# A two-layer diffusion trunk on one core: weights laid out in tile order by the host, and mirrored token tiles gathered by row numbers

## The chip, the core and the metric

The kernel runs on one core of a Trainium2 chip. The core has five engines that run their own instruction streams: TensorE (PE, matrix products; its weight loads are PEld), VectorE (DVE), ScalarE (ACT), GpSimd (POOL) and SyncE (SP), which here only issues DMAs. Sixteen DMA engines move data between the device memory (DRAM) and the on-chip memory. The metric is the device time of one execution in microseconds, and the median of the runs is taken.

## What is computed

The reference is a trunk of two layers over 512 latent tokens of 1024 features, with 256 context tokens. Layer 0 mixes tokens with a bidirectional state-space model (S5) on half of the features and neighbourhood attention on the other half; layer 1 mixes with a two-dimensional Fourier transform and a linear map. After each mixer there is a squared-ReLU MLP with 4096 hidden features. Cut to what matters here:

```python
def fourier_mix(h, w_f):
    hf = jnp.fft.fft2(h.astype(jnp.float32), axes=(1, 2), norm='ortho').real
    return hf.astype(h.dtype) @ w_f

def sqrelu_mlp(x, w1, w2):
    return jnp.square(jax.nn.relu(x @ w1)) @ w2

    # in each layer (sh, sc, g: slices of silu(c) @ w_mod[layer] + b_mod[layer])
        hl = modulate(rms_norm(h, norm_g[layer, 0]), sh1, sc1)
        ...                                  # out_l: S5 and attention, or fourier_mix(hl, w_fourier)
        h = h + g1[:, None, :] * rms_norm(out_l, norm_g[layer, 1])
        hf = modulate(rms_norm(h, norm_g[layer, 2]), sh2, sc2)
        h = h + g2[:, None, :] * rms_norm(sqrelu_mlp(hf, w_ff1[layer], w_ff2[layer]), norm_g[layer, 3])
```

All of it is float32.

## The kernel before

Every float32 product is made of three products in PE's float32r format: each operand is split into a high part and a low rest, and `mm3` (L105 to L108) adds high times high, high times low and low times high. Weights stream through the on-chip memory in chunks of 1 MB, a tile of 128 partitions by 2048 numbers. `Weights.pair` issues the load on SP (L54), lets ACT cast the high part (`whi`, L66) and DVE subtract it for the low part (`wlo`, L70). For some chunks (five of `w_in`, one of `w_out`, chunk 0 of `w_ff1` in each layer) ACT writes the negative high part (L68) and a DMA that POOL issues (L72) adds the weights onto it a second time from DRAM, in place of DVE. A chunk is cut from the plain matrix, so a partition's 8 KB come as eight rows of 1 KB (`w_in`, `w_ff1`) or four of 2 KB (`w_glu`, `w_out`, `w_ff2`). The modulation columns of the first norm (`wm`, L272) come as sixteen loads of 512 KB, in rows of 512 bytes.

The order of the instructions on each engine is chosen by a scheduler that simulates the program when it is built; each engine then runs its own list in that order. A DMA on SP or POOL is issued in the order of that engine's list, too.

The Fourier mixing of layer 1 is written with half-size transforms that use mirror symmetries. At the end of the first MLP each of the four token tiles of the residual `h` is written to DRAM (`hd`, L1137, in `fold`), normed into the tile `mf`, and folded on DVE (L1112 to L1117, L1145; a memset of one column by POOL, L1147). `stage1` (L1160, L1171) multiplies the folds by a token table into the PSUM tiles `pst`, then `feat` (L1213, L1215) multiplies by a feature table (`td<-tabD`, L1190) into `pa` and `pn`. Their results are split into `abh` and `abl`, and first columns are kept as `nyc` (L1224). `ny` is the split last row (`stack3`, L1074 to L1082). `stage3` multiplies by the linear map into `pq` and `pp` (L106 to L108, and L1264 with `ny`).

The map is used in four parts q = 0 to 3 of 256 columns, as the sums and differences of its rows l and 1024 - l. `mapw` loads a part with five DMAs, rows of `w_fourier` and of its reversed copy `wfr` (L1090 to L1093), and a memset (L1094); takes the difference `ws` (L1098) and the sum (L1101), on DVE for q = 1 and on POOL for the others; splits both (L183); and loads one more row (L1105). Part 1 goes into a piece of the tile `td`, part 3 (`w`, the tile `w3`) into the room of `mf`.

The mixing's output leaves in an order in which half of the tokens are mirrored (tokens 256, 511, 510 and so on). So the residual is brought into that order: a DRAM copy `hr` of the second half in reverse (L1184) is read back into tiles 1 and 3 of `h` (L1249, L1250, L1252); tiles 0 and 2 are read from `hd` (L1248, L1251).

Of the kernel before, what the change touches and what calls it, by code (L numbers as in the profile page):

```python
# [34 lines left out]
class Weights:  # L35
    """Streams float32 weights in chunks and splits each exactly into two float32r parts."""
# [23 lines left out]
    def pair(self, src, n0, n1, pair=None, dma=False, parts=1):  # L60
        """dma: the low part is summed by a DMA, where VectorE is short of time."""
# [32 lines left out]
def trunk(tc, I, out, dump=None):  # L94
# [15 lines left out]
    with es:  # L110
# [7 lines left out]
        def psum(**bufs):  # L118
            """Cuts the PSUM banks anew: the number of each kind."""
# [18 lines left out]
        # ------------------------------------------------ constants  # L138
# [32 lines left out]
        def rstd(src, junk):  # L171
            """1 / rms of the rows of src [128, 1024]; junk is overwritten."""
# [40 lines left out]
        def gemv_row(p, layer, slot, dst, norm, plus):  # L213
            """dst [128, 1024], on every partition: (vector (+ 1)) * gain of that norm."""
# [18 lines left out]
        def gemv_cols(p, layer, slot, dst, b, g):  # L233
            """dst [128, 8], feature-major: the vector, or (vector + 1) * gain."""
# [11 lines left out]
        # ------------------------------------------------ layer 0  # L246
# [9 lines left out]
        def win(i):  # L256
            return W.pair(I["w_in"][0, :, i * 256:(i + 1) * 256].rearrange("(k p) n -> p k n", p=128), 8, 256,
                          dma=i in (5, 6, 7, 2, 3), parts=4)
# [35 lines left out]
        with pool("s5t", side="right") as st:  # L294
# [41 lines left out]
            # the rotation of 8 steps, as a fraction of 2^32; backward rows turn the other way  # L336
# [45 lines left out]
        # ------------------------------------------------ norm, modulation, S5's input  # L382
# [12 lines left out]
        def mod_cols(k):  # L395
            """Ac, Bc of feature block k: the block's modulation for both streams."""
# [120 lines left out]
        # ------------------------------------------------ S5: 8 blocks of 4 groups  # L517
        st_ = {}

        def s5_params(b):  # L520
            """Chunk operators of block b: transposed input map Qt, readout CA, local convolution M, rotations R."""
# [12 lines left out]
            if b in (1, 3, 5):  # before the queries come  # L534
# [57 lines left out]
        def s5_scan(b):  # L592
            """Runs block b: chunk inputs, scan over chunks, readout."""
# [85 lines left out]
        # ------------------------------------------------ neighbourhood attention  # L679
# [94 lines left out]
        def glu_weights():  # L774
            wo["glu"] = W.pair(I["w_glu"].rearrange("(k p) n -> p k n", p=128), 4, 512)
# [10 lines left out]
        # ------------------------------------------------ the rest of it, GLU  # L786
# [45 lines left out]
        def wout(i, pair=None):  # L832
            hf, kk = divmod(i, 2)
            return W.pair(I["w_out"][kk * 512:kk * 512 + 512, hf * 512:hf * 512 + 512]
                          .rearrange("(k p) n -> p k n", p=128), 4, 512, pair, i == 0, parts=2 if i < 3 else 1)
# [16 lines left out]
        # ------------------------------------------------ output projection, MLPs, Fourier mixing  # L852
# [9 lines left out]
        def residual(t, src, G, early=False):  # L862
            """h[t] += rms_norm(src) * gate, the gains folded into G; src is overwritten."""
# [17 lines left out]
        def halves(t):  # L881
            """A [128, 4104] tile as [half of the tokens, feature block, token]."""
# [42 lines left out]
        def load1(layer, c, dma=False):  # L925
            return W.pair(I["w_ff1"][layer, :, c * 256:(c + 1) * 256].rearrange("(k p) n -> p k n", p=128), 8, 256,
                          dma=dma)

        def load2(layer, p_, hf):
            return W.pair(I["w_ff2"][layer, p_ * 512:(p_ + 1) * 512, hf * 512:(hf + 1) * 512]  # L930
                          .rearrange("(k p) n -> p k n", p=128), 4, 512)

        # output projection, with the first MLP's input following each token tile
# [491 lines left out]
```

## Time and profile before

| | |
|---|---|
| median of 3 runs | 1275.31 us |
| the runs | 1271.62, 1275.31, 1276.59 us |
| span of the profiled execution | 1266.4 us |
| mean TensorE clock granted in it | 0.971 |
| PE busy | 1172.3 us (93%) |
| DVE, ACT, POOL busy | 794.3, 502.8, 100.6 us |
| moved by DMA | 171.76 MB in 127259 packets, of which 90956 under 2 KB |

The span runs from the first to the last instruction of one execution that the hardware profiler recorded, and all views below are of it. The median of the timed runs is 8.9 us longer than that span. PE is the busiest engine; where it is idle, the profile says which instruction it waited for and which engine or DMA released it.

### The profile page before, as it was taken

Reading aid. Unit: us, or ns where it says so; the run is one execution under the profiler, and the core shown is the slowest. Engines: PE = TensorE matmul, PEld = TensorE weight load, DVE = VectorE, ACT = ScalarE, POOL = GpSimd, SP = SyncE. Lnnn points to the kernel's source line nnn. Section 1 sums busy time; section 2 is a strip of 40 time slices with the busy share of each in tenths; the row PEclk is TensorE's granted clock in tenths of the full one; section 3 lists DMA queues with packets and bytes.
Section 4 is the critical chain, followed back from the end, with each engine's and each line's share of the span. In section 5 each row is a group of like instructions: output and inputs, shape, how many; then the busy total and the mean of one; then the engine's idle time right before and its main releaser. Section 6 shows DMA issues by size and latency. Waiting matters only on the chain.

```text
span 1266.4 us, 15594 instructions
## 1 busy us (share of the span) xinstructions
PE 1172.3 (93%) x6090; PEld 963.7 (76%) x6090; DVE 794.3 (63%) x1233; ACT 502.8 (40%) x827; POOL 100.6 (8%) x164
## 2 busy tenths in 40 slices
PE   5999999899999999999999999428799999999997
PEld 2688888678977888888888877217788888888886
DVE  7657998789567666766756468045674444444445
ACT  6755554457726542322322232125744223223221
POOL 2001012000013000000000023013200000000002
PEclk8999999999999999999999999768899999999999
DMA  9757446304749356555555323322364322223201
GB/s 274 171 146 169 107 97 104 100 15 166 244 173 286 126 193 220 175 179 196 174 188 170 100 67 105 109 96 94 79 210 155 100 95 80 92 100 100 100 1 67
DMA packets 127259, 171.76 MB, mean 136 GB/s; under 512 B 17739, under 2 KB 90956, under 8 KB 127184
## 3 DMA queue, kind: packets, MB, share of 16 engines
q1 hardware_dynamic: 118480, 160.65, 39.8%
q0 software_dynamic: 7808, 8.39, 4.3%
q10 hardware_dynamic: 896, 1.72, 0.4%
q8 instruction: 48, 0.79, 0.2%
q14 instruction: 27, 0.22, 0.1%
HBM read 164.45 MB, written 7.49 MB: 136 GB/s over the span
## 4 chain that ended last, share of the span: by engine, by line
PE 76%; DVE 9%; DMA 5%; ACT 3%; SPq 3%; issue 1%; POOL 1%; DVEq 0%; POOLq 0%; ACTq 0%
PE pf L106 9%; PE pf L108 9%; PE pf L107 9%; PE pff L106 9%; PE pff L108 9%; PE pff L107 9%; SPq L1092 2%; DMA wlo<-w_ff 1%; PE po L746 1%; PE pq L108 1%; PE pq L106 1%; DMA wlo<-w_in 1%; PE pq L107 1%; PE po L106 1%; PE po L108 1%
## 5 line engine op out<-in xcount | busy, mean ns | idle before, releaser
L66 ACT CAST whi<-wraw 128x2048 fp32r<-128x2048 f32 (+2 forms) x103 | 147.7, 1457 | 306.3 <-PE pff L108 175.3
L70 DVE TENSOR_TENSOR wlo<-wraw,whi 128x2048 fp32r<-128x2048 f32 (+2 forms) x79 | 156.9, 1993 | 116.4 <-ACT whi L66 116.3
L106 PE MATMUL pff<-whi,ah 128*128 128x512 f32 (+1 forms) x482 | 189.4, 394 | 1.2 <-DVE facc L1011 1.2
L108 PE MATMUL pff<-whi,al 128*128 128x512 f32 (+1 forms) x482 | 189.2, 393 | 0.0
L107 PE MATMUL pff<-wlo,ah 128*128 128x512 f32 (+1 forms) x482 | 188.9, 393 | 0.0
L1011 DVE TENSOR_TENSOR facc<-facc,pff 128x512 f32<-128x512 f32 (+1 forms) x113 | 76.6, 680 | 91.4 <-PE pff L108 91.4
L207 DVE SCALAR_TENSOR_TENSOR gacc<-wraw,cs,gacc 128x1024 f32<-128x1024 f32 x76 | 97.4, 1282 | 28.1 <-DMA wraw<-w_mod 24.6
L108 PE MATMUL pf<-f1fh,wlo 128*128 128x512 f32 (+1 forms) x288 | 105.7, 371 | 4.5 <-DMA wlo<-w_ff 4.5
L106 PEld LDWEIGHTS pff<-whi,ah 128*128 128x128 f32 x482 | 90.5, 188 | 22.9 <-DVE facc L1011 1.6
L107 PE MATMUL pf<-f1fl,whi 128*128 128x512 f32 (+1 forms) x288 | 106.1, 372 | 0.9 <-DVE f1fl L908 0.9
L106 PE MATMUL pf<-f1fh,whi 128*128 128x512 f32 (+1 forms) x288 | 105.0, 373 | 1.9 <-ACT f1fh L183 0.9
L108 PEld LDWEIGHTS pff<-whi,al 128*128 128x128 f32 x482 | 90.5, 188 | 21.3
L107 PE MATMUL pf<-f0fl,whi 128*128 128x512 f32 (+1 forms) x288 | 105.6, 371 | 1.0 <-DVE f0fl L908 1.0
L107 PEld LDWEIGHTS pff<-wlo,ah 128*128 128x128 f32 x482 | 90.6, 188 | 20.8
L108 PE MATMUL pf<-f0fh,wlo 128*128 128x512 f32 (+1 forms) x288 | 105.2, 369 | 1.2 <-DMA wlo<-w_ff 1.2
L106 PE MATMUL pf<-f0fh,whi 128*128 128x512 f32 (+1 forms) x288 | 103.8, 372 | 0.7 <-ACT rl L995 0.7
L995 ACT ACTIVATE rl<-pf 128x512 f32<-128x512 f32 (+1 forms) x72 | 39.0, 547 | 117.0 <-PE pf L108 110.5
L997 DVE TENSOR_TENSOR rl<-rl 128x512 f32<-128x512 f32 (+1 forms) x72 | 46.6, 651 | 58.1 <-ACT ah L996 52.7
L108 PEld LDWEIGHTS pf<-f1fh,wlo 128*128 128x128 f32 x288 | 54.5, 190 | 14.8 <-DMA wlo<-w_ff 4.7
L106 PEld LDWEIGHTS pf<-f1fh,whi 128*128 128x128 f32 x288 | 53.7, 190 | 12.7 <-ACT f1fh L183 1.1
L108 PEld LDWEIGHTS pf<-f0fh,wlo 128*128 128x128 f32 x288 | 54.0, 188 | 11.4 <-DMA wlo<-w_ff 1.4
L107 PEld LDWEIGHTS pf<-f1fl,whi 128*128 128x128 f32 x288 | 54.3, 189 | 10.9 <-DVE f1fl L908 1.1
(476 smaller groups left out, 2251.4 us busy)
## 6 DMA issues: line engine op xcount, KB each, us to landing
wraw<-w_ff SPq DMA_DIRECT2D x64, 1024.0 KB
wraw<-w_mod SPq DMA_DIRECT2D x40, 1024.0 KB
wm<-w_mod SPq DMA_DIRECT2D x16, 512.0 KB
wraw<-w_in SPq DMA_DIRECT2D x8, 1024.0 KB
wlo<-w_in POOLq DMA_DIRECT2D x5, 1024.0 KB, 9.3
wraw<-w_out SPq DMA_DIRECT2D x4, 1024.0 KB
BC<-s5bc SPq DMA_DIRECT2D x16, 128.0 KB
M<-kd SPq DMA_DIRECT2D x32, 64.0 KB
```

Of the source, the lines that this page charges most:

```text
L66: self.nc.scalar.copy(hi[:, k], t[:, k])
L70: self.nc.vector.tensor_tensor(lo[:, k], t[:, k], hi[:, k].bitcast(F32), SUB)
L106: T.matmul(ps, lh, rh, start=start, stop=False)
L107: T.matmul(ps, lh, rl, start=False, stop=False)
L108: T.matmul(ps, ll, rh, start=False, stop=stop)
L207: V.scalar_tensor_tensor(acc, w[:, j], cw, acc, MULT, ADD)
L746: T.matmul(outs[ct][:, h], pTs[i % 2][0:kn, j], vv[:, h * 64:h * 64 + 64], start=(j == 0), stop=(j == 3))
L995: A.activation(rl, pf, AF.Relu)
L997: V.tensor_tensor(rl, rl, rl, MULT)
L1011: V.tensor_tensor(dst, dst, pt, ADD)
L1092: SY.dma_start(wv[:, 1], I["wfr"][255:511:2, cols])
```

## The change

Three things change. The host lays `w_in`, `w_glu`, `w_out`, `w_ff1`, `w_ff2` and the modulation columns (a new array `mod0`) out in the order of the tiles, so that each partition reads one run of 8 KB, and the modulation columns come in eight loads of 1 MB instead of sixteen of 512 KB. The host also lays out the parts of the Fourier map (`map`): one load of 1 MB takes the place of the five loads and the memset. And the reversed copy `hr` goes away: tiles 1 and 3 of `h` are gathered from `hd` by two indirect DMAs that POOL issues, with row numbers from the host (`rev`). Comments go too, so line numbers shift by a few. The core of the diff:

```diff
     def win(i):
-            return W.pair(I["w_in"][0, :, i * 256:(i + 1) * 256].rearrange("(k p) n -> p k n", p=128), 8, 256,
-                          dma=i in (5, 6, 7, 2, 3), parts=4)
+            return W.pair(I["w_in"][i].rearrange("p (k n) -> p k n", k=8), 8, 256, dma=i in (5, 6, 7, 2, 3), parts=4)
...
             wm = wmp.tile([128, 8, 2, 128], F32, tag="wm", name="wm", bufs=2)
-            for s_, slot in enumerate((1, 0)):
-                mod_load[:] = [SY.dma_start(wm[:, :, s_], I["w_mod"][0, :, slot * D + k * 128: slot * D + (k + 1) * 128]
-                             .rearrange("(k p) n -> p k n", p=128))]
+            mod_load[:] = [SY.dma_start(wm, I["mod0"][k].rearrange("p (k s n) -> p k s n", k=8, s=2))]
...
         def load1(layer, c, dma=False):
-            return W.pair(I["w_ff1"][layer, :, c * 256:(c + 1) * 256].rearrange("(k p) n -> p k n", p=128), 8, 256,
-                          dma=dma)
+            return W.pair(I["w_ff1"][layer, c].rearrange("p (k n) -> p k n", k=8), 8, 256, dma=dma)
...
             wr, wv = t[:, 0:4], t[:, 4:8]
-            for o in range(2):
-                SY.dma_start(wr[:, 2 * o:2 * o + 2], WF[o:512:2, cols].rearrange("(k p) n -> p k n", p=128))
-            SY.dma_start(wv[1:128, 0], I["wfr"][1:255:2, cols])
-            SY.dma_start(wv[:, 1], I["wfr"][255:511:2, cols])
-            SY.dma_start(wv[:, 2:4], I["wfr"][0:511:2, cols].rearrange("(k p) n -> p k n", p=128))
-            P.memset(wv[0:1, 0], 0.0)
+            SY.dma_start(t, I["map"][q].rearrange("p (k n) -> p k n", k=8))
...
         fold(3)
-        SY.dma_start(hr.rearrange("t (o d) -> o t d", o=2), hd[257:512].rearrange("t (o d) -> o t d", o=2)[:, ::-1])
...
         SY.dma_start(h[:, 0], hd[0:128])
-        SY.dma_start(h[0:1, 1], hd[256:257])
-        SY.dma_start(h[1:128, 1], hr[0:127])
         SY.dma_start(h[:, 2], hd[128:256])
-        SY.dma_start(h[:, 3], hr[127:255])
+        for t in range(2):
+            P.indirect_dma_start(out=h[:, 2 * t + 1], out_offset=None, in_=hd[:, :],
+                                 in_offset=bass.IndirectOffsetOnAxis(ap=rev[:, t:t + 1], axis=0))
...
+    a["rev"] = np.stack([np.where(p == 0, 256, 512 - p), 384 - p], -1).astype(np.uint32)
+    wf = np.concatenate([i["w_fourier"][0], np.zeros((1, D), np.float32)])
+    ls = np.concatenate([even, odd])
+    wf2 = np.concatenate([wf[ls], wf[1024 - ls]])
+    a["map"] = chunks(wf2, 8, 256)[0]
```

The scheduler sees another program, so the lists of the engines change in places. On SP, before, at the Fourier mixing (`td<-w_fourier` and `td<-wfr` are part 1 of the map, `w_6884` part 3; part 2 was issued earlier):

```order
L1190 DMA td<-tabD 128x2x1026
L1090 DMA td<-w_fourier 128x2x256 x2
L1091 DMA td<-wfr 127x256
L1184 DMA hr<-hd 2x255x512
L1092 DMA td<-wfr 128x256
L1093 DMA td<-wfr 128x2x256
L1248 DMA h<-hd 128x1024
L1251 DMA h<-hd 128x1024
L1250 DMA h<-hr 127x1024
L1252 DMA h<-hr 128x1024
L1090 DMA w_6884<-w_fourier 128x2x256 x2
L1091 DMA w_6884<-wfr 127x256
```

And SP there now:

```order
L1178 DMA td<-tabD 128x2x1026
L1083 DMA td<-map 128x2048
L1236 DMA h<-hd 128x1024
L1237 DMA h<-hd 128x1024
L1083 DMA w_6861<-map 128x2048
L54 DMA wraw_7144<-w_ff 128x2048
L1094 DMA w_6850<-wmid 1x256
```

Between the feature table and part 3 of the map stand three issues instead of ten, and nothing of `hr`.

POOL, before, at the same place (the `mf` memset is that of the last token tile; `wraw_6856` is part 2 of the map, `w_6884` part 3):

```order
L1147 MEMSET mf 128x1
L1075 MEMSET s_6780 65x260
L1075 MEMSET s_6848 65x260
L1098 TENSOR_TENSOR ws<-wraw_6856 128x1024
L1094 MEMSET w_6884 1x256
L1099 MEMSET ws 1x256 x2
L1101 TENSOR_TENSOR wraw_6856<-wraw_6856 128x1024
L1075 MEMSET s_6876 65x260
L1098 TENSOR_TENSOR ws<-w_6884 128x1024
L1075 MEMSET s_6904 65x260
L1099 MEMSET ws 1x256
L1101 TENSOR_TENSOR w_6884<-w_6884 128x1024
```

POOL now:

```order
L1239 DMA h<-hd,rev 128x1024 x2
L1136 MEMSET mf 128x1
L1069 MEMSET s_6762 65x260
L1069 MEMSET s_6830 65x260
L1087 TENSOR_TENSOR ws<-wraw_6838 128x1024
L1088 MEMSET ws 1x256 x2
L1090 TENSOR_TENSOR wraw_6838<-wraw_6838 128x1024
L1069 MEMSET s_6853 65x260
L1087 TENSOR_TENSOR ws<-w_6861 128x1024
L1088 MEMSET ws 1x256
L1090 TENSOR_TENSOR w_6861<-w_6861 128x1024
L1069 MEMSET s_6876 65x260
```

The two gathers stand ahead of the memset of `mf`, and so of everything that POOL does in this stage.

DVE, before, where it prepares `ny` (`s_6848` is its sum; `gn` are row sums that use `nyc`; `wlo_6892` is the low part of part 3):

```order
L1244 TENSOR_SCALAR gn<-wraw_6362,nyc 128x256
L1244 TENSOR_SCALAR gn<-td,nyc 128x256
L1244 TENSOR_SCALAR gn<-wraw_6856,nyc 128x256
L1081 TENSOR_TENSOR s_6848<-pn,rh 1x258
L1242 SCALAR_TENSOR_TENSOR gn<-wraw_6362,nyc,gn 128x256
L1242 SCALAR_TENSOR_TENSOR gn<-td,nyc,gn 128x256
L1242 SCALAR_TENSOR_TENSOR gn<-wraw_6856,nyc,gn 128x256
L1242 SCALAR_TENSOR_TENSOR gn<-wraw_6362,nyc,gn 128x256
L183 TENSOR_TENSOR wlo_6892<-ws,whi_6891 128x1024
```

DVE now (`s_6830` is the sum for `ny`, `wlo_6864` the low part of part 3):

```order
L1230 SCALAR_TENSOR_TENSOR gn<-wraw_6355,nyc,gn 128x256
L183 TENSOR_TENSOR abl<-pa,abh 128x258
L1212 COPY nyc<-pa 128x1
L1230 SCALAR_TENSOR_TENSOR gn<-td,nyc,gn 128x256
L183 TENSOR_TENSOR abl<-pa,abh 128x256
L1230 SCALAR_TENSOR_TENSOR gn<-wraw_6838,nyc,gn 128x256
L183 TENSOR_TENSOR wlo_6864<-ws,whi_6863 128x1024
L1075 TENSOR_TENSOR s_6830<-pn,rh 1x258
L1232 TENSOR_SCALAR gn<-w_6861,nyc 128x256
```

Three row sums and the first low part of part 3 have moved ahead of the sum for `ny`.

## Rows read from the trace of the kernel before

**Rows 1.** The page, part 1: busy time and share of each engine.

```profile
PE 1172.3 (93%) x6090; PEld 963.7 (76%) x6090; DVE 794.3 (63%) x1233; ACT 502.8 (40%) x827; POOL 100.6 (8%) x164
```

**Rows 2.** PE's waits: engine, line, releaser; us in all, times, longest.

```profile
PE pp L1264 <- ACT ny L1082: 23.1, 1, 23.1
PE pa L1213 <- DVE nyc L1224: 22.7, 1, 22.7
PE gp L412 <- ACT wmh L403: 9.5, 1, 9.5
PE pf L108 <- DMA wlo<-w_ff: 5.6, 2, 4.5
PE pq L108 <- DMA wlo<-w_in: 5.1, 1, 5.1
```

**Rows 3.** Windows: length; busy of each engine; PE clock, DMA share, GB/s.

```profile
20.00:40.00 20.00, 18.67 (x78) 8.82 (x77) 18.97 (x52) 13.69 (x26) 1.98 (x3) 0.88 0.84 226
...
430.00:560.00 130.00, 130.00 (x581) 106.00 (x580) 89.23 (x92) 46.03 (x54) 2.88 (x3) 1.00 0.56 186
```

**Rows 4.** Timeline of SP's DMA issues: start, us, line, tile, count.

```profile
745.43 1.86 SPq L1092 DMA_DIRECT2D wraw<-wfr  x1
...
785.65 1.50 SPq L1190 DMA_DIRECT2D td<-tabD  x1
...
790.63 5.45 SPq L1184 DMA_DIRECT2D hr<-hd  x1
...
796.13 17.53 SPq L1092 DMA_DIRECT2D td<-wfr  x1
...
839.98 9.51 SPq L1092 DMA_DIRECT2D w<-wfr  x1
```

**Rows 5.** Windows, the Fourier stage.

```profile
796.00:814.00 18.00, 10.13 (x42) 6.38 (x41) 0.97 (x5) 3.87 (x9) 0.30 (x1) 0.89 0.13 50
...
823.30:837.10 13.80, 7.91 (x32) 5.14 (x33) 13.65 (x23) 7.09 (x14) 3.72 (x4) 0.62 0.23 78
...
862.00:882.00 20.00, 20.00 (x145) 17.55 (x145) 14.55 (x27) 10.54 (x23) 5.24 (x6) 0.93 0.34 107
```

**Rows 6.** The chain that ended last: start, us, what.

```profile
30.61 5.52 DMA wraw<-w_in
...
785.03 5.53 DMA hd<-h
...
813.70 9.49 DMA td<-wfr
...
849.54 7.12 DMA w<-wfr
```

**Rows 7.** Timeline of DVE, 797 to 866 us.

```profile
798.19 0.41 DVE L1201 COPY p<-pst 1x258 f32<-1x258 f32 x1
...
823.31 1.23 DVE L1098 TENSOR_TENSOR ws<-td 128x1024 f32<-128x1024 f32 x1 [24.70 <-DMA td<-wfr]
...
825.83 2.45 DVE L1081 TENSOR_TENSOR s<-w,rh 1x256 f32<-1x256 f32 x1
...
860.76 2.30 DVE L183 TENSOR_TENSOR wlo<-ws,whi 128x1024 fp32r<-128x1024 f32 x1 [21.96 <-ACT whi L183]
...
862.98 0.47 DVE L1242 SCALAR_TENSOR_TENSOR gn<-td,nyc,gn 128x256 f32<-128x256 f32 x1
```

**Rows 8.** Timeline of PE, the last row of stage 1.

```profile
798.69 0.39 PE L1171 MATMUL pst<-zero 1*128 1x512 bf16 x1
```

**Rows 9.** Timelines of POOL and ACT, part 3 of the map.

```profile
859.62 2.35 POOL L1101 TENSOR_TENSOR w<-w 128x1024 f32<-128x1024 f32 x1
...
859.68 1.05 ACT L183 CAST whi<-ws 128x1024 fp32r<-128x1024 f32 x1 [23.45 <-POOL ws L1099]
```

**Rows 10.** Line L72, the accumulating DMAs: issue ns, and landing.

```profile
L72 POOL DMA_DIRECT2D wlo<-w_in x5: 1553/1561/1732, 102.4 to 212.0; - x5
...
DMA to landing us min/median/max: 8.8/9.3/14.7
```

More of the change, by code (lines that the diff above doesn't have):

```diff
@@ L774, in glu_weights @@
         def glu_weights():
-            wo["glu"] = W.pair(I["w_glu"].rearrange("(k p) n -> p k n", p=128), 4, 512)
+            wo["glu"] = W.pair(I["w_glu"].rearrange("p (k n) -> p k n", k=4), 4, 512)
             yield
@@ L832, in wout @@
         def wout(i, pair=None):
-            hf, kk = divmod(i, 2)
-            return W.pair(I["w_out"][kk * 512:kk * 512 + 512, hf * 512:hf * 512 + 512]
-                          .rearrange("(k p) n -> p k n", p=128), 4, 512, pair, i == 0, parts=2 if i < 3 else 1)
+            return W.pair(I["w_out"][i].rearrange("p (k n) -> p k n", k=4), 4, 512, pair, i == 0,
+                          parts=2 if i < 3 else 1)
         def side_gen():
@@ L925, in load1 @@
         def load1(layer, c, dma=False):
-            return W.pair(I["w_ff1"][layer, :, c * 256:(c + 1) * 256].rearrange("(k p) n -> p k n", p=128), 8, 256,
-                          dma=dma)
+            return W.pair(I["w_ff1"][layer, c].rearrange("p (k n) -> p k n", k=8), 8, 256, dma=dma)
         def load2(layer, p_, hf):
-            return W.pair(I["w_ff2"][layer, p_ * 512:(p_ + 1) * 512, hf * 512:(hf + 1) * 512]
-                          .rearrange("(k p) n -> p k n", p=128), 4, 512)
+            return W.pair(I["w_ff2"][layer, p_, hf].rearrange("p (k n) -> p k n", k=4), 4, 512)
         om = acc_tile("om")
@@ L1052, in trunk @@
         hd = drp.tile([S, D], F32, name="hd")
-        hr = drp.tile([255, D], F32, name="hr")
         hv = hd.rearrange("(r c i) d -> c r i d", c=8, i=8)
+        rev = rw.tile([128, 2], U32, name="rev")
         alt = rw.tile([1, 258], F32, name="alt")
@@ L1062, in tables @@
             SY.dma_start(alt, I["alt"])
+            SY.dma_start(rev, I["rev"])
             P.memset(zero, 0.0)
@@ L1066, in tables @@
             mapw(0, [t.rearrange("p (k n) -> p k n", k=8) for t in halves_(big("fl", F32R, "w0", 4104))])
-        WF = I["w_fourier"]
         wq, plus = {}, {}
@@ L1104, in mapw @@
             w5 = small_tile(F32, "w5")[0:1, 0:256]
-            SY.dma_start(w5, WF[512:513, cols])
+            SY.dma_start(w5, I["wmid"][:, cols])
             wn = rw.tile([65, 256], F32R, tag="wn", name="wn", bufs=4)
@@ L1340, in prepare, with chunks @@
     a["norm_g"] = f(i["norm_g"])
-    a["w_in"] = f(i["w_in"])
+    def chunks(w, k, n):
+        r, c = w.shape[-2] // (k * 128), w.shape[-1] // n
+        w = w.reshape(*w.shape[:-2], r, k, 128, c, n)
+        m = w.ndim - 5
+        return f(w.transpose(*range(m), m, m + 3, m + 2, m + 1, m + 4).reshape(*w.shape[:m], r, c, 128, k * n))
+    a["w_in"] = chunks(i["w_in"][0], 8, 256)[0]
+    m0 = chunks(i["w_mod"][0][:, 0:2 * D], 8, 128)[0].reshape(2, 8, 128, 8, 128)
+    a["mod0"] = f(m0[::-1].transpose(1, 2, 3, 0, 4).reshape(8, 128, 2048))
     a["ident"] = np.eye(128, dtype=np.float32)
@@ L1372, in prepare @@
     a["mask"] = mk.reshape(128, 3, 4, 64)
-    a["w_glu"] = f(i["s5_w_glu"][0])
-    a["w_out"] = f(i["w_out_even"][0])
+    a["w_glu"] = chunks(i["s5_w_glu"][0], 4, 512)[0, 0]
+    a["w_out"] = f(chunks(i["w_out_even"][0], 4, 512).transpose(1, 0, 2, 3).reshape(4, 128, 2048))
     d, i2 = np.arange(256), np.arange(257)
@@ L1395, in prepare @@
     a["alt"] = al
-    a["wfr"] = f(i["w_fourier"][0][:512:-1])
-    a["w_fourier"] = f(i["w_fourier"][0])
-    a["w_ff1"] = f(i["w_ff1"])
-    a["w_ff2"] = f(i["w_ff2"])
+    p = np.arange(128)
+    a["rev"] = np.stack([np.where(p == 0, 256, 512 - p), 384 - p], -1).astype(np.uint32)
[3 more added lines that the diff above has]
+    a["map"] = chunks(wf2, 8, 256)[0]
+    a["wmid"] = f(i["w_fourier"][0][512:513])
+    a["w_ff1"] = chunks(i["w_ff1"], 8, 256)[:, 0]
+    a["w_ff2"] = chunks(i["w_ff2"], 4, 512)
     a["s5d"] = f(i["s5_d"][0].reshape(32, 16).T)
```

## The prediction

> **What bounds the kernel now.** I read the page first, for who is busy; then PE's waits, for what it lacks the rest of the time; then the windows, to see in which stages that matters; then SP's own rows and the chain of waits around the places found.
>
> PE is busy 1172.3 of 1266.4 us [rows 1]: 94.1 us of idle are all that a change of loads can win, since PE's instructions stay what they are. Its waits name two of 23.1 and 22.7 us, one at 9.5, and two on DMAs that add up the low weight parts, 5.6 and 5.1 [rows 2]. The windows show where loads are already hidden: in 430–560 us, where the first MLP streams its weights, PE is busy 130.00 of 130.00 with the DMA engines at 0.56 [rows 3]. There, a faster load changes when a buffer fills, and nothing else. What counts is the Fourier stage (785–862 us), and less the first 40 us, where DVE is busy 18.97 of 20.00 [rows 3].
>
> The Fourier stage, from SP's rows [rows 4]: behind the tabD load stand the pieces of map part 1 (L1090 to L1093) with the mirrored copy of the residual (L1184) between them. L1184 is issued at 790.63 and takes the queue 5.45 us; the next issue, L1092 for 128x256, holds it 17.53 us. The same L1092 took 1.86 us at 745.43. So SP isn't waiting for data, its issue is stuck behind the copy. In 796–814 the 16 DMA engines are busy 0.13 [rows 5]: no lack of bandwidth, but a transfer on few engines (two would be 0.125). The chain goes on with the last piece's landing at 813.70 + 9.49, and DVE's `ws`, idle for 24.70 us, at 823.31 [rows 6, 7]. That is the 22.7 us wait. The second is like it: with the copy read back (L1250, L1252) ahead of it, map part 3 is issued in pieces until 849.5, L1092 again for 9.51 us [rows 4]; it lands after 7.12 us at 856.66 [rows 6], and POOL and ACT make `ny` for PE's 23.1 us wait.
>
> **The change part by part.**
>
> *The map in one load, no copy.* SP's tabD issue ends at 787.15 [rows 4], and part 1 follows it at once. For a landing the rows give 5.52 us (1 MB of `w_in`, in rows of 1 KB), and 7.12 and 9.49 for the last piece of a map part [rows 6]; with 7 it lands near 794.6, with the worst at 797. DVE gets to `ws` when its copy to `p` is done, 798.19 + 0.41 = 798.6 [rows 7]. So either way the load is hidden behind stage 1, and DVE starts 24.7 us earlier. If that cover were gone, each us beyond 798.6 would cost one.
>
> Part 3's load needs the buffer of `mf`, which PE's last stage-1 row releases at 798.69 + 0.39 = 799.1 [rows 8]. SP has two straight loads of `h` before it, then issues it; it lands at 804.6 to 808.6 instead of 856.66. POOL's difference and sum cost 2.35 each, ACT's cast of each 1.05 [rows 9]: `ny` could be made 6.8 later, at 811.4 to 815.4.
>
> What is late next is DVE. From 823.31 to 837.10 it was busy 13.65 of 13.80 us with the two map operations, the `abl` and `wlo` splits and the row sums [rows 5]. The same work now starts at 798.6. Against it: one of its operations, `s`, took 2.45 beside a POOL pass; a copy of its size takes 0.41 [rows 7], −2.0. For it: the order puts `wlo` of part 3 (2.30) and three more row sums (0.47 each [rows 7]) in front of the `s` for `ny`, which ended this stretch. That makes 13.8 − 2.0 + 2.3 + 1.4 = 15.5, so 814.1; with the cast to `ny`, 0.4, and a us and a half for handovers, PE passes L1264 near 816 rather than 861.1 (856.66, POOL's 2.35, and 2 us of memset and casts). **45 us**. Ends: 48 if DVE's passes are as short as alone and only part 3, at 812 to 813, binds; 35 if each of the some ten handovers between PE, ACT, POOL and DVE, until now slack, costs a us.
>
> *Clock.* While PE waited, its granted clock fell: 0.62 in 823–837, and still 0.93 in the 20 us after 862 [rows 5], where PE had no idle. 7% of 20 us is 1.4. A shorter gap gives back some of this: **1** (0 to 1.4).
>
> *Gathers.* Two indirect gathers of 128x1024 stand on POOL, ahead of the `mf` memset that stage 1's last quarter reads, and of both map passes. They wait for the last write to `hd`, 785.03 + 5.53 = 790.6 [rows 6]. No row shows a gather. The nearest is POOL's issue of a 1 MB accumulating DMA, 1553 to 1732 ns [rows 10]: a gather moves half the bytes but reads its row numbers first. I take that, 1.6 each; the memset then runs at 793.8, and of stage 1's last quarter, which ends at 799.1, only the last matmuls read it. After it POOL has two passes of 2.35 and some memsets to do before part 3 lands: done by 801. So **0**, hidden behind stage 1 and part 3's load. Bounds: at nothing it is still 0; at 5 us each the memset comes at 800.6, PE ends stage 1 some 4 us later, and that is paid.
>
> *Accumulating DMAs.* Five with `w_in`, two with `w_ff`, one with `w_out`, landing in 8.8 to 14.7, median 9.3 us [rows 10]. Only three were waited for. Their source rows grow from 1 KB to 8 KB. The nearest row of longer pieces is the same transfer with 2 KB rows, `w_out`, the 8.8: 0.5 per landing, so for the two of `w_ff` **1** (0 to 5.6). The `w_in` wait of 5.1 belongs to the one landing of 14.7, 5.4 above the median, so something shared the engines; in its window that may repeat. **3** (0 to 5.1).
>
> *Start.* The modulation columns came in 512 KB loads of 512-byte rows, and PE waited 9.5 us for the first [rows 2]. Now one 1 MB load in 8 KB rows. The 9.5 hold the load and ACT's cast of the tile; with no cast and a load of 5.52 [rows 6] the most to win is 4.0. The least is 0, since DVE paces the next 20 us with work of its own [rows 3] and starts earlier only if the tokens, loaded behind the columns, come earlier. The middle: **2** (0 to 4).
>
> *The other weights* (`w_ff`, the rest of `w_in`, `w_glu`): **0** by [rows 3]: the loads lie under PE's matmuls, and the largest wait on a plain weight load isn't among PE's first five [rows 2].
>
> Sum: 45 + 1 + 0 + 1 + 3 + 2 + 0 = 52. Span 1266.4 − 52 = 1214.4. The median of the runs, 1275.31, lies 8.9 above the span, so **1223 us**.
>
> **The rivals.**
>
> *Squeeze.* What PE waits for becomes DVE, ACT and POOL working back to back, at 35 us for the stage. For it: [rows 7] show `s` at 2.45 beside POOL's pass, and POOL's passes now all fall into DVE's. Against: DVE was 99% busy in 823–837 with the same neighbours. Time 1223 + 10 = 1233.
>
> *Slow gathers.* Each 5 us or more on POOL, with `mf` and both map passes behind them: 4 to 6 us lost, 1228. For it: they are POOL's first piece of work after a wait, with row numbers to read. Against: of five issues of the accumulating kind none took over 1732 ns [rows 10]. The Trainium skill (DMA: Bandwidth & Descriptors, section SWDGE vs HWDGE vs iDMA) has a rule that speaks for this rival and against the change: descriptors issued from GpSimd are written to rings in SBUF, which DVE can lock GpSimd out of, while SP's loads are immune. By that rule the gathers could hang while DVE folds tile 3, an estimated 2 to 3 us, and the sum would be 49 to 52; the trace shows no such delay for the issues it has.
>
> *Slower.* The same gathers at such a price that they eat all: POOL's four passes of 2.35 after them, with memsets and casts, are some 13 us, so PE passes L1264 at 790.6 + T + 13 against 861.1, with 7 us won elsewhere: from T = 64, 32 us each, it is no faster than before, 1275; at 36 each 1283. That is a gather that takes 250 ns or more for each of its 128 rows.
>
> *Half the stall stays.* Part 3's load lands late, since SP issues it only after a wait on PE, ACT and POOL, and weight loads queue with it: at 20 us instead of 5.5 to 9.5, 1237 to 1245.
>
> *All waits on loads go.* 22.7 + 23.1 + 9.5 + 5.6 + 5.1 = 66 [rows 2], and 1 of clock: 1208. Against it: DVE's 15.5 us stay, whoever loads.
>
> *The change doesn't do what it says*, because the stuck issue is a slow queue and not the copy: then L1092's 17.53 would turn up in another place, 1270. Against: 1.86 for the same issue without the copy ahead [rows 4].
>
> **How the numbers follow.** Forecast 0.55; squeeze 0.15; slow gathers 0.12; half the stall 0.07; all waits gone 0.06; no change 0.02; slower 0.03. The time is the forecast's, 1223. From 1208 (all waits gone) to 1242 (squeeze, slow gathers and the milder end of half a stall) about 0.85 to 0.9 lies. Within 0.5% (6 us), about what a measurement of this kernel can tell from no change, is only the no-change case: faster 0.95, same 0.02, slower 0.03.
>
> **What would show it.** SP: part 1's load issued within 1 us of tabD's, no issue above 3 us in 785–815. DVE's `ws` at 798 to 800, not 823. PE's two waits of 23 gone, with one of up to 10 in their place, on `ny` or on a `wlo` by DVE. POOL: two gather issues between 790 and 794 of 1 to 2 us, and PE's stage 1 ending at 799. The streaming stages, 430–560 and from 935 on, moved by the gain and otherwise as before. Wrong it would be with a gather of over 5 us, a wait for part 3's map above 10, or a streaming stage in which PE's idle time changed.

## The result

The changed kernel took 1234.22 us (median of 4 runs, 1229.26 to 1236.31) beside 1273.46 us for the kernel before in the same comparison: a ratio of 0.970, 95% interval 0.9663 to 0.9738, so 39 us faster where 52 were forecast. 1223 was 11 us too low; the range of 1208 to 1242 held.

The page of the changed kernel, busy times and the DMA packets:

```profile
PE 1175.5 (95%) x6090; PEld 967.0 (79%) x6090; DVE 793.4 (64%) x1233; ACT 502.4 (41%) x827; POOL 99.1 (8%) x162
...
DMA packets 50936, 170.72 MB, mean 139 GB/s; under 512 B 17571, under 2 KB 22184, under 8 KB 38446
```

The packets went from 127259 to 50936, most of it by the new layout (55066 in e1, below, which has the layout alone). What PE waits for now (engine, line, releaser; us in all, times, longest):

```profile
PE gp L409 <- ACT wmh L400: 9.1, 1, 9.1
PE pf L108 <- DMA wlo<-w_ff: 7.6, 2, 4.5
PE pn L1201 <- DVE nyc L1212: 4.9, 1, 4.9
PE ptx L422 <- DVE xt L389: 4.2, 5, 1.2
...
PE pq L108 <- DMA wlo<-w_in: 2.8, 1, 2.8
PE py L644 <- DMA M<-kd: 2.4, 1, 2.4
...
PE pst L1149 <- POOL mf L1136: 1.3, 1, 1.3
```

Both waits of 23 us [rows 2] are gone; in their place stand 4.9 on `nyc` and 1.3 on POOL's memset of `mf`. Of the waits that the layout was to shorten, the one on the first modulation columns is 9.1 for 9.5, the one on the accumulated `w_ff` 7.6 for 5.6, and the one on `w_in` 2.8 for 5.1. Two others grew: on the normed input tokens `xt`, 4.2 for 0.9, and on a small load of layer 0's state-space model (`M`), 2.4 for nothing.

SP's issues in the Fourier stage (start, us, line, tile):

```profile
791.99 1.48 SPq L1178 DMA_DIRECT2D td<-tabD  x1
793.52 1.48 SPq L1083 DMA_DIRECT2D td<-map  x1
...
805.71 0.33 SPq L1083 DMA_DIRECT2D w<-map  x1
```

Part 1 of the map follows the table at once and no issue takes above 1.5 us, where [rows 4] had 5.45, 17.53 and 9.51. DVE's rows there:

```profile
805.05 0.41 DVE L1189 COPY p<-pst 1x258 f32<-1x258 f32 x1
805.39 1.20 DVE L1087 TENSOR_TENSOR ws<-td 128x1024 f32<-128x1024 f32 x1
...
807.89 2.47 DVE L1075 TENSOR_TENSOR s<-w,rh 1x256 f32<-1x256 f32 x1
...
812.26 6.68 DVE L183 TENSOR_TENSOR wlo<-ws,whi 128x1024 fp32r<-128x1024 f32 x2
...
824.16 1.21 DVE L183 TENSOR_TENSOR wlo<-ws,whi 128x1024 fp32r<-128x1024 f32 x1
825.40 0.42 DVE L1075 TENSOR_TENSOR s<-pn,rh 1x258 f32<-1x258 f32 x1
```

`ws` starts right behind the copy to `p`, no longer 24.7 us later [rows 7]. But `s` takes 2.47 us, and two low parts take 6.68, where one took 1.21 at 824.16. POOL at the same time:

```profile
797.48 1.10 POOL L1239 DMA_INDIRECT h<-hd,rev  x1 [4.67 <-DMA hd<-h]
798.88 0.96 POOL L1239 DMA_INDIRECT h<-hd,rev  x1 [0.30 <-PE pst L1160]
799.85 0.12 POOL L1136 MEMSET mf<- 128x1 f32 x1
...
807.24 2.83 POOL L1090 TENSOR_TENSOR wraw<-wraw 128x1024 f32<-128x1024 f32 x1
...
811.68 2.89 POOL L1087 TENSOR_TENSOR ws<-w 128x1024 f32<-128x1024 f32 x1
...
814.90 2.96 POOL L1090 TENSOR_TENSOR w<-w 128x1024 f32<-128x1024 f32 x1
```

The gathers cost POOL 1.10 and 0.96 us. They come 7 us later than forecast from the start of the trace, as all of this stage does, and the memset behind them at 799.85 is what PE waited 1.3 us for. From 807 on POOL's passes over the map take 2.83 to 2.96 us, where [rows 9] had 2.35 (the one that ran beside DVE's `s` in the kernel before, at 825.12, had taken 2.87). Windows of the streaming stage, of the Fourier stage, and of the 20 us behind it:

```profile
430.00:560.00 130.00, 130.00 (x607) 107.19 (x606) 89.44 (x99) 46.91 (x58) 2.23 (x3) 1.00 0.53 182
806.00:828.00 22.00, 17.07 (x68) 12.19 (x69) 21.84 (x31) 12.49 (x26) 10.06 (x8) 0.77 0.28 108
828.00:848.00 20.00, 20.00 (x156) 17.79 (x155) 12.86 (x27) 11.29 (x25) 6.11 (x6) 1.00 0.30 107
```

430–560 is at 130.00 of 130.00, as in [rows 3], with the DMA engines at 0.53 instead of 0.56. After the Fourier stage the clock is at 1.00 instead of 0.93 [rows 5]. Within it, it had fallen all the same: to 0.50, the 1.2 GHz level, in the 6 us from 821.7 to 827.7, after PE's 4.9 us on `nyc`.

To compare the traces I read four marks in PE's timeline of each kernel: A, the first matmul of the MLP's second product; B, the end of stage 1; C, the matmul with `ny` (L1264 before); D, the end of PE's last row. In us from the start of the span:

```
kernel                       A        B        C        D     B-A    C-B    D-C
before                  442.61   799.08   861.09  1259.44   356.5   62.0  398.4
changed                 450.47   805.94   827.70  1224.39   355.5   21.8  396.7
e1 layout only          445.79   802.25   864.54  1262.78   356.5   62.3  398.2
e2 map and gathers      449.45   808.44   830.18  1228.60   359.0   21.7  398.4
e3 gathers + layout     447.04   804.06   831.04  1229.29   357.0   27.0  398.3
e4 map + layout         447.13   802.47   854.93  1253.27   355.3   52.5  398.3
e5 copy in 16 pieces    452.73   808.39   835.24  1248.17   355.7   26.9  412.9
e6 sums on VectorE      444.65   800.47   818.95  1215.58   355.8   18.5  396.6
e7 gathers late         448.92   804.22   824.94  1221.27   355.3   20.7  396.3
e8 w_ff low on VectorE  447.46   803.01   824.75  1218.92   355.6   21.7  394.2
e9 changed, again       450.08   809.16   830.91  1226.74   359.1   21.8  395.8
e10 = e6 + late gathers 454.00   808.13   826.87  1224.39   354.1   18.7  397.5
e11 = e10 + e8          443.92   798.05   816.79  1211.95   354.1   18.7  395.2
e12 copy of 256 rows    446.88   802.22   818.13  1215.09   355.3   15.9  397.0
```

The stretch from B to C belongs to the program: four profiles of kernels whose parts there are alike (changed, e2, e8, e9) have 21.7 to 21.8, two have 18.7. They agree better than their parts: in e2 and e9 PE comes to B at a clock of 0.50 and waits 2.1 and 0.6 us for `ny` at C, while in the first profile of the changed kernel it comes to C at 0.50 and waits for nothing there. Mark A does not belong to the program.

### The profile page after: what moved, and what is told of

The parts are those of the page before. It is cut to its first block, busy times and chain, and to the rows that moved or that the text cites. A ratio compares the mean times of both kernels' runs of the same rounds, so it can differ in the third digit from the quotient of the medians.

```text
span 1231.0 us, 15546 instructions
## 1 busy us (share of the span) xinstructions
PE 1175.5 (95%) x6090; PEld 967.0 (79%) x6090; DVE 793.4 (64%) x1233; ACT 502.4 (41%) x827; POOL 99.1 (8%) x162
## 2 busy tenths in 40 slices
DMA packets 50936, 170.72 MB, mean 139 GB/s; under 512 B 17571, under 2 KB 22184, under 8 KB 38446
## 4 chain that ended last, share of the span: by engine, by line
PE 81%; DVE 7%; DMA 4%; ACT 4%; issue 2%; SPq 1%; POOL 1%; DVEq 0%; POOLq 0%; ACTq 0%
PE pff L106 10%; PE pf L108 10%; PE pff L108 10%; PE pff L107 10%; PE pf L106 10%; PE pf L107 10%; DMA wlo<-w_ff 2%; PE pst L1149 2%; PE po L743 1%; SPq L685 1%; PE pq L106 1%; PE pq L108 1%; PE po L106 1%; PE po L108 1%; PE po L107 1%
```

## The experiments

Times are medians; a ratio is to the kernel before, timed beside it.

**e1, the layout alone** (map in five pieces, reversed copy kept):

```diff
-    a["map"] = chunks(wf2, 8, 256)[0]
+    a["wfr"] = f(i["w_fourier"][0][:512:-1])
...
+        SY.dma_start(hr.rearrange("t (o d) -> o t d", o=2), hd[257:512].rearrange("t (o d) -> o t d", o=2)[:, ::-1])
```

> The kernel before with the tile-order weights alone (w_in, w_glu, w_out, w_ff1, w_ff2, modulation columns); the Fourier map in its five pieces and the reversed copy of the residual stay. Theory (the layout costs time in the first half): PE reached the end of stage 1 of the Fourier mixing 6.9 us later in the changed kernel, so this kernel should be 5 to 8 us slower than before, and its two waits of 23 us stay. Rival (the delay came from the map and the gathers through the scheduler): within 2 us of before. Second rival (larger rows do help and something else hid it): 3 us or more faster.

1272.46 us (10 runs) beside 1270.63 (19): ratio 1.0009, 0.9987 to 1.0032. PE's longest waits in it:

```profile
PE pp L1258 <- ACT ny L1076: 23.8, 1, 23.8
PE pa L1207 <- DVE nyc L1218: 22.7, 1, 22.7
```

The rival within 2 us holds. Both waits stay and the stretch B to C is 62.3. The layout, with its larger rows and half as many loads of modulation columns, is worth nothing that ten runs can tell; a gain of 6 us, which the forecast had for it, would be 0.9953, outside the interval. It isn't the rows alone, though: up to mark A the scheduler also put DVE's, ACT's and PE's instructions in another order here than in the kernel before, and larger rows in the old order weren't run.

**e2, the map and the gathers alone** (all weights in the old layout):

```diff
-            return W.pair(I["w_in"][i].rearrange("p (k n) -> p k n", k=8), 8, 256, dma=i in (5, 6, 7, 2, 3), parts=4)
+            return W.pair(I["w_in"][0, :, i * 256:(i + 1) * 256].rearrange("(k p) n -> p k n", p=128), 8, 256,
+                          dma=i in (5, 6, 7, 2, 3), parts=4)
```

and so for the other weights.

> The changed kernel with all weights in the old layout: only the map in one load and the gathers are new. Theory (the Fourier stage alone gives the gain, about 42 us from the end of stage 1 to the linear map): span 1266.4 - 42 = 1224, 5 to 8 us under the changed kernel, with PE's times up to 700 us as in the kernel before. Rival (the layout has no cost): the same as the changed kernel within 2 us.

1232.31 us, ratio 0.9696 (0.9678 to 0.9714): the changed kernel's 0.970, so the rival again, and from B to C 21.7. My theory took a difference of one trace to another for one of kernels. Up to mark A, e2 has the instructions of the kernel before in the same order on every engine (but for one more load of 1 KB, `rev`, near the end of that stretch), and reached it at 449.45 instead of 442.61.

**e3, gathers with the map in five pieces**:

```diff
-            SY.dma_start(t, I["map"][q].rearrange("p (k n) -> p k n", k=8))
+            for o in range(2):
+                SY.dma_start(wr[:, 2 * o:2 * o + 2], WF[o:512:2, cols].rearrange("(k p) n -> p k n", p=128))
+            SY.dma_start(wv[1:128, 0], I["wfr"][1:255:2, cols])
...
```

> The changed kernel with the map in five pieces again; no reversed copy, gathers as in the changed kernel. Theory (the copy on two DMA engines blocked SP's queue, the pieces did not): no SP issue above 4 us in the Fourier stage, the two waits of 23 us stay away, and at most 5 us slower than the changed kernel. Rival (the pieces of 127 rows and of 512 strided rows are what is slow): an issue of 9 us or more remains, and 15 to 40 us slower than the changed kernel.

1237.69 us, ratio 0.9741 (0.9725 to 0.9758). SP in the Fourier stage:

```profile
795.60 6.94 SPq L1087 DMA_DIRECT2D td<-wfr  x1
...
809.62 4.66 SPq L1087 DMA_DIRECT2D w<-wfr  x1
```

The waits of 23 us stay away without the copy, as the theory has it. But I expected no issue above 4 us, and the one behind the piece of 127 rows still holds SP 6.94 and 4.66 us. That the piece is the reason is argued: in this run the same issue behind the same piece took 1.91 us at 749.85, and in the 6.9 us from 795.60 the DMA engines were busy 0.86, so other transfers filled them (in the 4.7 us from 809.6 they were at 0.24). B to C is 27.0, 5.2 more than with the map in one load, and the time is 5.4 us above e2's, 3.5 above the changed kernel's: at the edge of the 5 that I had allowed.

**e4, the map in one load with the reversed copy** (gathers replaced by the copy and its read-back):

```diff
-            P.indirect_dma_start(out=h[:, 2 * t + 1], out_offset=None, in_=hd[:, :],
-                                 in_offset=bass.IndirectOffsetOnAxis(ap=rev[:, t:t + 1], axis=0))
+        SY.dma_start(h[1:128, 1], hr[0:127])
...
+        SY.dma_start(h[:, 3], hr[127:255])
```

> The changed kernel with the reversed copy and its read-back again instead of the gathers; map in one load. The list puts the copy behind part 1 of the map and its read-back ahead of part 3. Theory (the copy takes about 31 us, and what stands behind its read-back waits): the first wait of 23 us is gone, the second stays at 10 to 25 us, so 10 to 25 us slower than the changed kernel. Rival (the copy harms only by cutting the map's pieces apart): within 3 us of the changed kernel.

1262.62 us, ratio 0.9952 (0.9933 to 0.997): 28 us slower than the changed kernel, a little more than the 10 to 25 expected. SP's rows, and PE's longest wait:

```profile
790.25 1.55 SPq L1082 DMA_DIRECT2D td<-map  x1
793.30 0.67 SPq L1172 DMA_DIRECT2D hr<-hd  x1
794.01 17.96 SPq L1236 DMA_DIRECT2D h<-hd  x1
...
820.52 0.25 SPq L1238 DMA_DIRECT2D h<-hr  x1
```

```profile
PE pp L1252 <- ACT ny L1075: 38.5, 1, 38.5
```

Whatever stands behind the copy is held: here a plain load of `h`, 17.96 us, where it was a piece of the map for 17.53. The read-back is issued at 820.5, 27 us after the copy. The first wait is gone, since part 1 now stands ahead of the copy; the second grew to 38.5, where I had 10 to 25. Together with e3: without the copy but with the pieces 33 us are gained, with the map in one but the copy left 8, with both 38 (e2). The copy was the stall, and the pieces the smaller part of it.

**e5, the kernel before with the copy cut into 16 column pieces**:

```diff
-        SY.dma_start(hr.rearrange("t (o d) -> o t d", o=2), hd[257:512].rearrange("t (o d) -> o t d", o=2)[:, ::-1])
+        SY.dma_start(hr.rearrange("t (o d) -> o t d", o=16), hd[257:512].rearrange("t (o d) -> o t d", o=16)[:, ::-1])
```

> The kernel before with one change: the reversed copy of the residual cut into 16 column pieces (16x255x64) instead of 2 (2x255x512), so 16 DMA engines can share it, in pieces of 256 bytes. Theory (the stall behind the copy comes from two engines having it all to do; in the kernel before it took about 31 us at a DMA share of 0.13): the issue behind the copy takes under 8 us instead of 17.53, the read-back is issued 10 us or more earlier than 822, and the kernel is 10 to 35 us faster than before. Rival (the copy is slow for its count of rows or its reversed direction, on whatever number of engines): the issue behind it stays above 15 us and the time is that of before or worse, since there are 8 times as many pieces.

1250.27 us, ratio 0.9826 (0.9782 to 0.987): 21 us from one number. SP:

```profile
801.36 4.83 SPq L1184 DMA_DIRECT2D hr<-hd  x1
806.24 7.28 SPq L1092 DMA_DIRECT2D td<-wfr  x1
...
821.47 0.58 SPq L1250 DMA_DIRECT2D h<-hr  x1
822.09 11.99 SPq L1252 DMA_DIRECT2D h<-hr  x1
```

The issue behind the copy takes 7.28 instead of 17.53 us, and the read-back goes out 13.1 us after B instead of 23.1. In the 7.3 us from 806.2 the DMA engines are busy 0.67, where they had 0.13. Rows and bytes are the same as before, so it is the way the copy is cut over the engines that made the stall. The Trainium skill has the rule (DMA: Bandwidth & Descriptors, section Why a DMA increments its semaphore by 16 and not by 1): the largest number up to 16 that divides the slowest dimension of both sides is the number of engines, 2 for 2x255x512, 1 for 127 rows. The traces agree with it: in the kernel before, a share of 0.13 of 16 engines behind the copy [rows 5] and of 0.06, one engine, in the 8.8 us behind the 127 rows of L1250 (issued there at 822.18), and 0.67 in this run. The stall then moved on: L1250, 127 rows, goes out at 821.47, and the issue behind it, L1252, takes 11.99 us; the row loads of the map come late, and PE waits on row sums:

```profile
PE p L1278 <- DVE gn L1242: 14.0, 1, 14.0
...
PE pp L1264 <- ACT ny L1082: 5.7, 1, 5.7
```

That 14.0 is why D-C is 412.9 here, and why B to C gains 35 us and the time 21.

**e6, the sums and differences of parts 2 and 3 on VectorE**:

```diff
-            E_ = V if q == 1 else P
+            E_ = P if q == 0 else V
```

> The changed kernel with the sums and differences of map parts 2 and 3 on VectorE instead of GpSimd. In the changed kernel DVE took 6.68 us for two low parts and 2.47 for a one-row sum while POOL worked (alone 1.2 each and 0.42), 6.3 us more than alone. Theory (the two engines slow each other): DVE gets four passes of 1.22, 4.9 us, more, and its rows lose the 6.3, so PE passes the linear map 1 to 3 us earlier, or 3 to 5 with POOL's handovers gone. Rival (DVE is the bound and gets more work): 3 to 5 us slower.

1228.45 us, ratio 0.9669 (0.9624 to 0.9714); beside the changed kernel's 0.970 the time alone tells nothing. The trace does: DVE there,

```profile
801.07 1.21 DVE L1087 TENSOR_TENSOR ws<-wraw 128x1024 f32<-128x1024 f32 x1
...
803.44 0.41 DVE L1075 TENSOR_TENSOR s<-w,rh 1x256 f32<-1x256 f32 x1
...
805.43 1.22 DVE L183 TENSOR_TENSOR wlo<-ws,whi 128x1024 fp32r<-128x1024 f32 x1
...
816.34 1.21 DVE L183 TENSOR_TENSOR wlo<-ws,whi 128x1024 fp32r<-128x1024 f32 x1
```

has `s` at 0.41 and low parts at 1.21 or 1.22 each, and B to C falls from 21.8 to 18.5, by 3.3, although DVE does four passes more. The two engines slowed each other. Of the 3.3, DVE's list gives 2.0: counted from B, the `s` for `ny` ends after 17.9 us, in the changed kernel after 19.9. The rest is PE's own way to C, at a clock of 1.00 from B to C here and of 0.78 there. The Trainium skill (SBUF — State Buffer, section SBUF: two separate sides) has it that the ports they share are locked by one for a whole instruction, while the other waits. The rows of the changed kernel agree: `s`, begun at 807.89, ended at 810.36, 0.3 us after POOL's pass of 807.24 + 2.83.

**e7, the gathers behind POOL's last pass**; no other row moves on any engine:

```diff
-            E_.tensor_tensor(wr, wr, wv, ADD)
+            fo["sum"] = E_.tensor_tensor(wr, wr, wv, ADD)
...
+        with behind(fo["sum"]):
```

> The changed kernel with the two gathers issued behind POOL's last map pass; no other row moves on any engine. Theory (the gathers hold the memset that stage 1 reads, PE waited 1.3 us for it, and POOL's passes start 2 us later): 1 to 3 us faster from the end of stage 1 on; the wait of PE on POOL's memset is gone. Rival (hidden): no difference from the changed kernel, and the memset wait turns into one on SP's or DVE's work.

1230.83 us, ratio 0.9689 (0.9644 to 0.9734), not to be told from the changed kernel by time. POOL:

```profile
793.96 0.10 POOL L1136 MEMSET mf<- 128x1 f32 x1 [2.70 <-DVE eo L1131]
...
816.30 1.89 POOL L1240 DMA_INDIRECT h<-hd,rev  x1 [0.17 <-issue]
818.50 0.97 POOL L1240 DMA_INDIRECT h<-hd,rev  x1 [0.31 <-issue]
```

Counted from A, the memset comes 4.3 us earlier. PE's wait on it is gone, but 0.9 on DVE came in its place, and A to B takes 355.3 us as against 355.5: there the rival is right. B to C is 20.7, 1.0 less. That is within the theory's 1 to 3 us, but not for its reason: the `s` for `ny` ends 20.0 us after B, as in the changed kernel (19.9), and what is shorter is PE's way to C, at a clock of 0.84 instead of 0.78.

**e8, the low part of chunk 0 of `w_ff1` on VectorE**:

```diff
-                w1[0] = load1(0, 0, True)
+                w1[0] = load1(0, 0)
...
-                w1[0] = load1(1, 0, True)
+                w1[0] = load1(1, 0)
```

> The changed kernel with the low part of chunk 0 of the first MLP weights, in both layers, made by VectorE instead of the accumulating DMA. PE waited 7.6 us for these two landings (11.7 and about 9 us long). Theory (the landing is the wait): VectorE needs 2.3 us, so 3 to 8 us faster. Rival (VectorE is busy there and its other work comes late): within 2 us, or slower.

1233.64 us, ratio 0.9706 (0.9663 to 0.975): no difference. The waits on the landings are gone from its trace, waits on DVE's `f1fl` (1.9) and `f0fl` (1.5) came, and D-C is 394.2, 2.5 less than the changed kernel's 396.7. Below what the runs tell.

**e9, the changed kernel again.**

> The changed kernel itself, unaltered, as the measure for the next runs and for how much of its first half differs from one profiled execution to the next. Theory (the first half varies by the DMAs' timing, since kernels with the same lists on all engines reached the same place at 442 us up to 10 us apart): its time up to the end of stage 1 differs from the first profile of it by 2 us or more, and its span by a few us, while the stretch from the end of stage 1 to the linear map stays within 1 us of 21.8. Rival (the first half is fixed by the program): the same to 0.5 us everywhere.

1233.36 us (6 runs), ratio 0.9675 (0.9647 to 0.9702). A at 450.08, 0.4 from the first time; B 3.2 later; B to C 21.75, the first time 21.76. The numbers are as the theory has them, but the 3.2 us didn't come from the first half: two executions of one program happened to agree to A. That A varies stands on e2 and e5, which up to there equal the kernel before (e2 but for `rev`) and came 6.8 and 10.1 us later. The 3.2 us lie in stage 1, at PE's wait on the memset; the row behind it, and windows of 8 and 7 us:

```profile
800.08 1.13 PE L1149 MATMUL pst<-wraw,mf 128*128 128x256 f32 x4 [1.73 <-POOL mf L1136]
```

```profile
795.00:803.00 8.00, 6.28 (x29) 4.28 (x28) 1.78 (x8) 0.19 (x1) 5.00 (x6) 0.94 0.98 354
803.00:810.00 7.00, 7.00 (x19) 3.78 (x18) 3.32 (x7) 1.87 (x4) 1.22 (x3) 0.50 0.59 205
```

PE idled 1.73 us there (1.27 the first time), and the granted clock fell to 0.50, the 1.2 GHz level; from that row to B took 9.1 us. In the first profile the same rows ran at 1.00 and took 5.9. The length of the wait doesn't decide it: of the six profiles with a wait on this memset, e2's fell to 0.50 after 1.26 us, and the other four, with 1.27 to 1.63 (e6), stayed at 1.00. The two that fell have A to B at 359, and all others, with this wait or without, at 354 to 357. So a wait of 1.3 to 1.7 us can cost 3 us more by the clock, in some executions; what decides it no run shows.

**e10, e6 with the gathers behind POOL's memsets for part 3; e11, e10 with e8.**

```diff
-            P.memset(ws[0:1, 0], 0.0)
+            fo["sum"] = P.memset(ws[0:1, 0], 0.0)
```

and `with behind(fo["sum"])` as in e7.

> The changed kernel with the sums and differences of map parts 2 and 3 on VectorE, and the two gathers issued behind POOL's memsets for these parts instead of ahead of stage 1's memset. Theory (two engines slowing each other, and the memset held by the gathers, each cost some us): from the end of stage 1 to the linear map 18 to 19 us instead of 21.8, no PE wait on POOL's memset, and 4 to 6 us faster than the changed kernel, a ratio of 0.995 to 0.996 to it. Rival (VectorE's extra work makes this no gain): within 2 us.

> The one before this, with the low part of chunk 0 of the first MLP weights on VectorE as well. Theory (each wait of PE on an accumulating landing, 3 to 5 us in every profile, is a loss): another 2 to 6 us faster than the one before this. Rival (as in the run of that edit alone, whose time did not move): within 2 us of it.

e10 took 1224.62 us, ratio 0.9606 (0.9579 to 0.9633), apart from e9's interval: 8.7 us faster than the changed kernel, more than the 4 to 6 expected. B to C is 18.7, 3.0 less, B-A is 354.1, 5.0 less than in e9 and 1.4 less than in the first profile; PE has no wait from A to B. e11 took 1223.48, ratio 0.9617 (0.9592 to 0.9642): the rival, the same within 2 us, though D-C is 2.4 less.

**e12, no gathers**: the map in one load, and a copy of all 256 rows in 16 pieces, read back as tiles of 128 rows.

```diff
+        SY.dma_start(hr[0:1], hd[256:257])
+        SY.dma_start(hr[1:256].rearrange("t (o d) -> o t d", o=16), hd[257:512].rearrange("t (o d) -> o t d", o=16)[:, ::-1])
...
+        SY.dma_start(h[:, 1], hr[0:128])
...
+        SY.dma_start(h[:, 3], hr[128:256])
```

> No gathers: the map in one load, and the reversed copy with all 256 rows in DRAM, cut into 16 column pieces, and read back as whole tiles of 128 rows; the load of map part 3 stands ahead of the read-back. Theory (what costs is only that few engines do the copy and that its followers in SP's queue wait): within 5 us of the changed kernel. Rival (any reversed copy in SP's queue delays the map): 10 us or more slower, with a wait of PE above 10 us in the Fourier stage.

1225.79 us, ratio 0.9629 (0.9602 to 0.9657): by the medians 7.6 us faster than e9, where I expected at most 5 either way. The two intervals still touch (e9's begins at 0.9647). SP:

```profile
793.61 0.62 SPq L1173 DMA_DIRECT2D hr<-hd  x1
794.27 7.54 SPq L1237 DMA_DIRECT2D h<-hd  x1
...
802.45 0.33 SPq L1082 DMA_DIRECT2D w<-map  x1
```

The copy still holds its follower 7.54 us, with the DMA engines full this time (1.0), but part 1 is ahead of it, part 3 goes out at 802.45, only 0.2 us after B, and POOL is free of gathers. B to C is 15.9, the shortest of all: in this kernel's DVE list the sum for `ny` stands ahead of part 3's low part again, and its two low parts took 2.35 us, not 6.68, because POOL, which waited 2.3 us for part 3 to land, began its pass over it only at 810.26, near their end. That this order and not the missing gathers makes the difference to 20.7 (e7) is argued, not shown.

## Why the prediction was right or wrong

**What bounds.** Right. The Fourier stage was where time could be won, its two waits hung on SP's queue, and the copy on two engines held it (e4, e5).

**The Fourier term, 45.** Mechanism right, size 4.8 too large: B to C fell from 62.0 to 21.8, by 40.2. The step that failed is the line "15.5, so 814.1": from `ws` to the end of `s` DVE took 825.82 − 805.39 = 20.4 us. I had taken `s` down by 2.0 as if it were alone and priced the rest as before; `s` stayed at 2.47, and the two low parts took 6.68 instead of 2.4, beside POOL's passes. That is the squeeze rival, at 5 of its 10 us. e6 takes the contention away, and 3.3 us come back, 2.0 of them on DVE.

The last piece of that sum, 0.4 for the cast and a us and a half for handovers, measured 1.9 as forecast (825.82 to 827.70), but by luck: PE didn't wait for `ny`. It came late to C by itself, at a clock of 0.50 after its 4.9 us on `nyc`. Matmuls of the map before C, in the kernel before and now:

```profile
837.00 0.28 PE L106 MATMUL pp<-w,abh 128*128 128x256 f32 x1
837.12 0.28 PE L107 MATMUL pp<-w,abh 128*128 128x256 f32 x1
```

```profile
827.48 0.41 PE L108 MATMUL pq<-w,abl 128*128 128x256 f32 x1
827.70 0.41 PE L1252 MATMUL pp<-wn,ny 65*128 65x256 f32 x1
```

One started every 0.12 us then, and every 0.21 us now; the row at C shows no wait. The forecast had no price for PE's own pace there. Where PE does wait for `ny` (e6, e12), C comes 0.55 us behind the end of `s`.

**Clock, 1.** The size is right in this profile, D-C being 1.7 less with the clock at 1.00 in the 20 us behind C, but that is luck: the fall had come before C. In e2 and e3, where PE waits 2.1 and 1.9 us for `ny` at C itself, the clock behind C is 0.91 and 0.90, and D-C is that of the kernel before (398.4 and 398.3).

**Gathers, 0.** The price was a little high (1.6 each; 1.10 and 0.96), but they weren't hidden: they wait for the last write of `hd`, and PE waits 1.3 to 1.7 us for the memset behind them, in two of six profiles with a fall of the clock (e9). The cover that I named, that only stage 1's last matmuls read the memset's column, was wrong: PE wanted it 7.2 us before the end of stage 1. The rule of the Trainium skill (DMA: Bandwidth & Descriptors, section SWDGE vs HWDGE vs iDMA) on descriptors that DVE holds up decided nothing: DVE was idle from 797.05 to 798.79 and from 798.96 on, so for nearly all of both gathers. Behind POOL's passes in e7, beside a busy DVE, they took 1.89 and 0.97.

**Start 2, accumulating DMAs 1 + 3.** Wrong: these 6 us are nothing in time (e1). One of the waits did shrink: on `w_in` the three profiles of the old layout have 4.9 to 5.1, those of the new one 1.8 to 2.8 (e6 4.4, in two waits). But the new layout, with the order that the scheduler made for it, waits 3.1 to 4.2 for `xt` and 0.9 to 4.6 for `M`, where the old one has at most 0.9 and nothing, so that PE's waits up to A sum to 31 to 36 us with either. That is the step that failed here: the forecast counted waits that shrink and none that grow. The modulation wait went from 9.5 to 9.1 only. The landings of the accumulating DMAs went from a median of 9.3 to 9.0 us, and the one for layer 0's `w_ff` took 11.66 where it had taken 9.81 (the chains of waits): half a us off each landing was read from one row, and a landing varies by more than that between executions.

**Other weights, 0.** Right.

**The base.** Each time lies about 2 us above the span of its own execution in all later runs (1232.99 and 1231.0 here). The 8.9 that I added from span to median was thus mostly the luck of that profile, which reached A earlier than any other of the 14. It did no harm to a difference of medians, but I read waits of a few us in it as things to win, while kernels with the same program up to there came 7 to 10 us later.

**A rival's price.** *Half the stall stays* doesn't come out of its rows alone: a load of 20 us lands at 819.1, and with the 6.8 behind it PE passes at 826 instead of 816, which is 1233 and not 1237 to 1245. The case didn't come up; e4 shows how it would look, with more of the stall.

Sum by the marks: 40.2 + 1.7 = 41.9, and 1.0 from A to B, beside 39 by the medians, with 3.5 to 5 us of interval on either side. Of the 13 us between 52 and 39, the Fourier term makes 4.8 and the layout's terms 6.

## What to carry to other kernels

When a DMA issue takes 5 us or more, look at the busy share of the DMA engines in it. If it is low (0.13 here), look at the transfer ahead of it in that queue and at the length of its slowest dimension: the time is charged to the follower, as here to an innocent piece of the map, and one number (16 for 2) gave back 21 us. If it is high (0.86 in e3, 1.0 in e12), the engines are full. Bigger rows for loads that already lie under busy matmuls gave nothing here, though they saved over half of the packets. Before pricing a wait of a few us, find a second profile of the same program: what differs between them can't be won by an edit, and what an edit takes from one wait can come back at another.

## What the runs showed that I had not expected

The stretch up to A varied from 442.6 to 452.7 us among kernels with the same program there, while B to C of the changed kernel repeated to 0.02 us, by different ways. After a wait of PE on the same memset the clock stayed at 1.00 in four profiles (1.27 to 1.63 us of wait) and fell to 0.50 in two (1.26 and 1.73), for about 3 us of time. POOL's issue of an accumulating DMA of 1 MB of `w_in` fell from 1.55 us or more [rows 10] to 0.87 to 1.08 with the new layout. And the version without gathers, on plain loads alone, at 1225.79 us, and the one with the map's sums on VectorE and late gathers, at 1224.62, had lower medians than both kernels, the latter with an interval apart from the changed kernel's; their combination was not run.
